# Two chunk pairs of the mixer's input and output products by seven products per unit, and a new order of the chunks around them

## The chip, the cores and the metric

One Trainium2 chip, one core of it. The metric is the device time of one execution in microseconds (us). Five engines work side by side and meet by semaphores: TensorE (PE; PEld is its weight load), VectorE (DVE), ScalarE (ACT), GpSimd (POOL) and SyncE (SP), which issues the DMAs of the weights.

## The reference, cut to what matters

A decoder layer for 256 tokens, width 2048, fp32: a SwiGLU FFN, a mixer, and a second SwiGLU FFN, each closed by `LayerNorm(alpha * x + sublayer(x))`. The mixer is where the change is:

```python
(c_q, c_kv, k_rope, q_nsa, k_c, v_c, k_s, v_s, k_w, v_w, g_nsa) = split_cols(x @ w_in[l], IN_SIZES)
o_mla = mla_attention(c_q, c_kv, k_rope, ...)      # latent attention, 8 heads
o_nsa = nsa_attention(q_nsa, k_c, v_c, ...)        # compressed, selected and window branches, 8 heads
mix = jnp.concatenate([o_mla, o_nsa], axis=-1) @ w_out[l]
x = layer_norm(DEEPNORM_ALPHA * x + mix, ln2_g[l], ln2_b[l])
```

`w_in` is 2048 x 3416: 512 columns c_q, 256 c_kv, 64 k_rope, 1024 q_nsa, six times 256 for the keys and values of the branches (compressed, selected, window), 24 gates. `w_out` is 2048 x 2048; its rows 0 to 1023 take the latent heads, its rows 1024 to 2047 the NSA heads. `compress` makes 15 keys and 15 values out of overlapping blocks of 32 tokens of k_c and v_c, with a 4096 x 256 weight each.

## The kernel before, in words

The 256 tokens are two tiles t of 128 rows. The activations stand transposed in pieces (k, t) of 128 x 128 and are the stationary operand; weights stream as 128 x 512. Every large product in fp32 is three matmuls (`mm3`: high by high, high by low, low by high), so each weight is split in two. A piece of weights is 128 x 1024, half a megabyte: two k's of a chunk of 512 columns. SP loads it into `raw` (5 buffers) or `sum` (3 buffers), ACT casts the high part `whi` (L91 in `split`) and DVE subtracts for the low part `wlo` (L92); `whi` and `wlo` have 6 buffers each, so the cast of a piece waits until TensorE is done with the piece that lay in its buffer six splits ago.

`gemm` makes one chunk for both tiles. `gemm2` makes two chunks at once and goes by units, a unit being a pair of k's by two chunks by two tiles. A normal unit is 8 products, 24 matmuls. A unit named in `seven` is 7 products, 21 matmuls, by sums: DVE makes sums of the weights (L293 to L295) and splits four tiles instead of two, sums of the activations are made once (`sums`, `parts`), and at the end three accumulations `p1`, `p5`, `p6`, `p7` are put together by one ACT copy and four DVE operations (L332 to L336) and added to the four results (L345). FFN chunks are done so already; in the mixer no product is.

The mixer runs after the first LayerNorm (`ln`, by steps that are spread among the matmuls): chunks of `w_in` in the order c_q (`fin_a`), `w_in_b` = c_kv, k_rope and gates (`fin_b`: RMS norm, rope, gates), the compressed keys and values (`fin_c`); then the latent queries, latent attention for heads 0 to 3, the selected branch, NSA queries and so on, and at last `w_out`. Small attention work is written as generators (`spawn`) that advance by `tick`, between pieces of the large products, so that their waits lie behind matmuls; `drain` runs all of them to their end. The order on PE and SP is the order in which the program is written. The order on DVE, ACT and POOL is made by the scheduler at build time and fixed. Each engine runs its list from the front.

`out_last` does the last chunks of `w_out` tile by tile, so that the second LayerNorm's work on tile 0 lies behind the matmuls of tile 1. `out_fin` adds a finished chunk to the residual y, `ln_stats` takes its statistics.

## Time and profile before

| | before |
|---|---|
| time, median of 3 runs | 1766.75 us (1765.04 to 1768.03) |
| the profiled execution: time, span of its instructions | 1766.0 us, 1764.3 us |
| TensorE busy | 1745.0 us, 99% of the span |
| VectorE busy | 1596.6 us, 90% |
| ScalarE busy | 997.8 us, 57% |
| GpSimd busy | 17.4 us, 1% |
| mean granted TensorE clock | 0.998 |
| mean DMA rate | 198 GB/s |

The profile is one execution. What lies outside the span is 1.7 us. A busy share is a mean over the whole program. The mixer with its two LayerNorms lies at about 690 to 1060 us of the span; there the shares of DVE and ACT are lower than in the FFNs.

### The profile page before, as it was taken

The page shows a single profiled execution, that of the slowest core. Times are in us where ns is not written, and L with a number is a line of the kernel's source. Part 1 is how long each engine was busy: PE and PEld are TensorE (multiplying, and loading weights), DVE is VectorE, ACT ScalarE, POOL GpSimd, SP SyncE. Part 2 cuts the span into 40 slices and gives each one's busy share as a digit, 9 for nine tenths or more (in the row PEclk, how much of TensorE's full clock was granted, in tenths as well). Part 3 has the DMA queues.
Part 4 walks back from the last instruction along what each step waited for, and adds up shares of the span by engine and source line. Part 5 has one row for each costly group of instructions (what it writes and reads, how often), then busy time and mean ns, then how long its engine had stood idle before and what let it go on. Part 6 is the DMA issues. An engine that isn't in the chain of part 4 may idle for free.

```text
span 1764.3 us, 22385 instructions
## 1 busy us (share of the span) xinstructions
PE 1745.0 (99%) x8018; PEld 1429.0 (81%) x8018; DVE 1596.6 (90%) x2121; ACT 997.8 (57%) x1324; POOL 17.4 (1%) x40
## 2 busy tenths in 40 slices
PE   9999999999999999999999999999999999999997
PEld 7888888888888888887788778888888888888886
DVE  7899999999999998766576679899999999999997
ACT  6656555575655565654555555565655565655651
POOL 0000000000000000000000001000000000000000
PEclk9999999999999999999999999999999999999999
DMA  9665656556567557546843355656556656566654
GB/s 335 219 209 176 209 200 203 192 189 211 196 197 230 193 177 255 182 143 210 300 153 120 123 176 171 211 179 198 196 193 224 203 185 209 196 196 216 203 197 162
DMA packets 103440, 350.01 MB, mean 198 GB/s; under 512 B 11152, under 2 KB 13728, under 8 KB 103328
## 3 DMA queue, kind: packets, MB, share of 16 engines
q1 hardware_dynamic: 102016, 344.37, 58.1%
q0 software_dynamic: 1312, 4.21, 0.8%
q8 instruction: 63, 1.03, 0.2%
q14 instruction: 49, 0.40, 0.1%
HBM read 346.44 MB, written 2.10 MB: 198 GB/s over the span
## 4 chain that ended last, share of the span: by engine, by line
PE 74%; DVE 17%; DMA 3%; issue 3%; ACT 2%; SPq 0%; POOL 0%; DVEq 0%; ACTq 0%; POOLq 0%
PE bank L97 23%; PE bank L98 23%; PE bank L96 23%; DVE wlo L92 8%; DVE sum L293 2%; DVE w L345 2%; ACT whi L91 1%; DMA raw<-in_ffn_w_down 1%; DVE sum L295 1%; DVE sum L294 1%; DMA raw<-in_ffn_w_up 1%; DVE tlo L448 1%; PE bank L1004 1%; DMA raw<-in_w_in 1%; PE bank L994 1%
## 5 line engine op out<-in xcount | busy, mean ns | idle before, releaser
L96 PE MATMUL bank<-whi,thi 128*128 128x512 f32 (+1 forms) x1958 | 771.9, 394 | 0.0
L97 PE MATMUL bank<-wlo,thi 128*128 128x512 f32 (+1 forms) x1958 | 761.2, 389 | 1.5 <-DVE wlo L92 1.4
L98 PE MATMUL bank<-whi,tlo 128*128 128x512 f32 (+1 forms) x1958 | 761.1, 389 | 0.0
L91 ACT CAST whi<-raw 128x1024 fp32r<-128x1024 f32 (+2 forms) x569 | 533.1, 965 | 264.7 <-PE bank L98 123.2
L92 DVE TENSOR_TENSOR wlo<-raw,whi 128x1024 fp32r<-128x1024 f32 (+2 forms) x569 | 624.0, 1111 | 63.6 <-ACT whi L91 62.9
L91 ACT CAST whi<-sum 128x1024 fp32r<-128x1024 f32 x267 | 279.2, 1050 | 369.3 <-DVE sum L295 143.2
L96 PEld LDWEIGHTS bank<-whi,thi 128*128 128x128 f32 x1958 | 368.0, 188 | 79.1 <-issue 5.4
L98 PEld LDWEIGHTS bank<-whi,tlo 128*128 128x128 f32 x1958 | 367.6, 188 | 76.5
L97 PEld LDWEIGHTS bank<-wlo,thi 128*128 128x128 f32 x1958 | 368.2, 188 | 75.8 <-DVE wlo L92 3.8
L92 DVE TENSOR_TENSOR wlo<-sum,whi 128x1024 fp32r<-128x1024 f32 x267 | 319.3, 1214 | 26.0 <-ACT whi L91 23.7
L97 PE MATMUL bank<-wlo,m 128*128 128x512 f32 x424 | 166.0, 392 | 2.0 <-DVE wlo L92 2.0
L96 PE MATMUL bank<-whi,m 128*128 128x512 f32 x424 | 165.1, 389 | 0.0
L98 PE MATMUL bank<-whi,m 128*128 128x512 f32 x424 | 165.1, 389 | 0.0
L293 DVE TENSOR_TENSOR sum<-raw 128x1024 f32<-128x1024 f32 x106 | 129.0, 1217 | 9.1 <-DMA raw<-in_ffn_w_down 5.0
L97 PEld LDWEIGHTS bank<-wlo,m 128*128 128x128 f32 x424 | 79.5, 188 | 22.3 <-DVE wlo L92 5.5
L96 PEld LDWEIGHTS bank<-whi,m 128*128 128x128 f32 x424 | 79.6, 188 | 16.6
L98 PEld LDWEIGHTS bank<-whi,m 128*128 128x128 f32 x424 | 79.6, 188 | 16.0
L345 DVE TENSOR_TENSOR w<-bank,w 128x512 f32<-128x512 f32 x120 | 78.7, 681 | 0.2
L295 DVE TENSOR_TENSOR sum<-sum,raw 128x512 f32<-128x512 f32 x106 | 72.3, 683 | 0.2
L294 DVE TENSOR_TENSOR sum<-sum,raw 128x512 f32<-128x512 f32 x106 | 72.3, 683 | 0.0
L733 ACT ACTIVATE w<-w,mx 128x256 f32<-128x256 f32 (+1 forms) x48 | 21.4, 446 | 29.8 <-DVE mx L729 28.1
L440 PEld LDWEIGHTS bank<-ident,w 128*128 128x128 f32 x176 | 21.9, 140 | 5.8
(190 smaller groups left out, 889.7 us busy)
## 6 DMA issues: line engine op xcount, KB each, us to landing
raw<-in_ffn_w_down SPq DMA_DIRECT2D x169, 512.0 KB, 4.7
raw<-in_ffn_w_up SPq DMA_DIRECT2D x160, 512.0 KB, 4.8
raw<-in_ffn_w_gate SPq DMA_DIRECT2D x146, 512.0 KB, 5.0
raw<-in_ffn_gu SPq DMA_DIRECT2D x32, 512.0 KB, 4.2
raw<-in_w_in SPq DMA_DIRECT2D x30, 512.0 KB, 5.1
raw<-in_w_out SPq DMA_DIRECT2D x20, 512.0 KB, 3.3
sum<-in_w_in SPq DMA_DIRECT2D x18, 512.0 KB, 5.4
sum<-in_ffn_w_gate SPq DMA_DIRECT2D x12, 512.0 KB, 4.1
```

The lines of the kernel that those rows point to most:

```text
L91: A.copy(hi, src)
L92: V.tensor_tensor(lo, src, f(hi), op=OP.subtract)
L96: PE.matmul(ps, xh, wh, start=first, stop=False)
L97: PE.matmul(ps, xh, wl, start=False, stop=False)
L98: PE.matmul(ps, xl, wh, start=False, stop=last)
L293: V.tensor_tensor(t13, a_, b_[:, 1:2, :].broadcast_to([P, 2, NCH]), op=OP.add)
L294: V.tensor_tensor(t24[:, 0], t13[:, 0], a_[:, 1], op=OP.add)
L295: V.tensor_tensor(t24[:, 1], t24[:, 0], b_[:, 0], op=OP.add)
L345: V.tensor_tensor(rest[b], B[b], rest[b], op=OP.add)
L440: PE.transpose(pt[:, j, :], hs[c, t][:, j * P:(j + 1) * P], ident)
L448: V.tensor_tensor(hT[c, t][1], src, f(hT[c, t][0]), op=OP.subtract)
L733: A.activation(s[:, h, :], s[:, h, :], AF.Exp, bias=mx[:, h:h + 1], accum_out=sm[:, h:h + 1])
```

## The change

- `w_in`: the chunk c_q and the chunk of the compressed keys and values become one pair, `w_in_a`, done by `gemm2` with units 4 and 5 by seven products. The first four units are done for tile 0 first, then for tile 1 (`head=4`). Before, c_q was a `gemm` with `head=8` and the other chunk came after `w_in_b`.
- The order after `w_in_b`: the compressing generators are spawned and the selected branch's chunk comes directly; then latent queries, the latent attention of heads 0 to 3, and the first NSA queries. Before: latent queries, latent attention, then the spawn and the selected branch.
- `w_out`: all four chunks are done for rows 0 to 1023 as before. For rows 1024 to 2047, columns 0 to 1023 become a pair `w_out_a` (`gemm2`, four units in the order 0, 1, 3, 2, of which 1 and 2 by seven products), and columns 1024 to 2047 are `w_out_b`, done whole in `out_last`. Before, rows 1024 to 1535 were done for all chunks, then came `drain`, rows 1536 to 2047 of chunk 0, and `out_last` did the other three.
- `drain` now runs in the pair, after its first unit (`mixed`), where the activations' sums for unit 2 are made too (`mix_sums`).
- `ln` makes the activations' sums of units 4 and 5 itself (`now_too`). The values of the second latent attention stand in a `sum` buffer.

```diff
+WIN, WIN7 = (0, 1, 2, 3, 4, 6, 5, 7), (4, 5)
+WOUT, WOUT7 = (0, 1, 3, 2), (1, 2)
...
+                    if now_too and len(u) == 4:
+                        xs[2 * n + j] = parts(sums(u))
...
-    gemm(xin, w_in, 0, KALL, fin_a, head=HEAD, spare=SPARE, nxt=(W["w_in_b"], 0, 0))
-    gemm(xin, W["w_in_b"], 0, KALL, fin_b, nxt=(w_in, 3, 0))
...
-    gemm(xin, w_in, 3, KALL, fin_c, nxt=(uq, 2, 0))
+
+    gemm2(xin, xs1, WIN, WIN7, "w_in_a", 0, lambda t, j, r: (fin_c if j else fin_a)(t, r), head=4,
+          nxt=(W["w_in_b"], 0, 0))
+    gemm(xin, W["w_in_b"], 0, KALL, fin_b, nxt=(w_in, 2, 0))
...
+    def out_last(w, ks):
 
         held = {}
         for t in range(NT):
-            for n in ns:
+            for n in range(2):
                 ps = new_bank()
                 if t == 0:
-                    held[n] = [(ks[i:i + KT], load(W["w_out"], n, ks[i:i + KT])) for i in range(0, len(ks), KT)]
+                    held[n] = [(ks[i:i + KT], load(w, n, ks[i:i + KT], n == 1 and i >= 4)) for i in range(0, len(ks), KT)]
...
-    gemm(lambda k, t: sl(cq[t], k), uq, 2, list(range(4)), fin_qr, nxt=(uq, 0, 0))
-    mla_att(*mla_proj(0, (w_in, 4, 0)))
     spawn(compress(kcT, "k"), "C")
     spawn(compress(vcT, "v"), "C")
     new_kv("sel")
-    gemm(xin, w_in, 4, KALL, fin_kv2("sel"), each=lambda i: ln_res("ln1", i // 2) if i % 2 else None,
-         nxt=(w_in, 1, 0))
+    gemm(xin, w_in, 2, KALL, fin_kv2("sel"), each=lambda i: ln_res("ln1", i // 2) if i % 2 else None, nxt=(uq, 2, 0))
+    gemm(lambda k, t: sl(cq[t], k), uq, 2, list(range(4)), fin_qr, nxt=(uq, 0, 0))
+    mla_att(*mla_proj(0, (w_in, 0, 0)))
...
-    out_proj(list(range(8)), range(4), True)
-    out_proj(list(range(8, 12)), range(4), False)
-    drain()
-    for n in range(1):
-        gemm(mixer, W["w_out"], n, list(range(12, 16)),
-             lambda t, ps: (out_fin(t, ps, n, False), ln_stats(t, n)))
-    out_last(list(range(12, 16)), (1, 2, 3))
+    for n in range(4):
+        gemm(mixer, W["w_out"], n, list(range(8)), lambda t, ps: out_fin(t, ps, n, True),
+             each=lambda i: mix_sums(1) if n == 3 and i == 2 else None)
+
+    def mixed(at):
+        if at == 0:
+            drain()
+            mix_sums(2)
...
+    gemm2(late_mix, xs3, WOUT, WOUT7, "w_out_a", 0, fin_o, each=mixed)
+    out_last(W["w_out_b"], list(range(8)))
```

In all there are 12 matmuls fewer, three for each of the four units of seven. The bytes loaded stay. The lines of `after` stand one to thirteen lines lower: `mm3` is L97 to L99, `split` L92 and L93, the sums L294 to L296, the putting together L333 to L337 and L348, the compressing matmuls L943, the softmax's transposes L774 and the products that follow them L1017, `out_fin` L1036.

Three places of the built order follow. First DVE, where the blocks for the first compressing matmuls are made (L919 before, L932 after). Before, at the end of the latent queries (L640 to L643 are rope, `wlo` the low parts of weights):

```order
L640 TENSOR_TENSOR w<-bank,pack 128x512
L643 TENSOR_TENSOR w<-w 128x512
L641 TENSOR_TENSOR w<-bank,pack 128x8x32
L642 TENSOR_TENSOR w<-bank,pack 128x8x32
L92 TENSOR_TENSOR wlo<-sum,whi 128x1024
L643 TENSOR_TENSOR w<-w 128x512
L92 TENSOR_TENSOR wlo<-sum,whi 128x1024 x2
L92 TENSOR_TENSOR wlo<-raw,whi 128x1024
L917 MEMSET w 128x32
L919 TENSOR_TENSOR w<-m,pack 128x16x15 x2
```

And after, right behind `w_in_b` (L659 to L662 the RMS norm of `fin_b`, L649 to L652 its rope, L689 to L692 the gates):

```order
L659 TENSOR_SCALAR ms<-ss 128x1
L93 TENSOR_TENSOR wlo<-raw,whi 128x1024
L687 COPY w<-w 128x64
L534 TENSOR_SCALAR rstd<-ms 128x1
L662 TENSOR_SCALAR w<-bank,rstd 128x256
L691 TENSOR_SCALAR gz<-gz 128x24
L684 MEMSET w 128x256
L692 RECIPROCAL gates<-gz 128x24
L649 TENSOR_TENSOR w<-bank,pack 128x64
...
L930 MEMSET w 128x32
L932 TENSOR_TENSOR w<-m,pack 128x16x15
```

The blocks have moved from behind rope and weight splits to behind the whole of `fin_b` for tile 1.

Second ACT, at the last softmax (L746 before, L756 after, scales the probabilities; L766 and L776 copy the transposed ones out of a bank; `whi` the high parts of weights). Before:

```order
L733 ACTIVATE w,sm<-w,mx 128x256 x2
L91 CAST whi<-sum 128x1024
L746 ACTIVATE w<-w,rs 128x256 x2
L91 CAST whi<-sum 128x1024
L766 COPY w<-bank 128x512
```

After, in the pair `w_out_a`:

```order
L92 CAST whi<-raw 128x1024
L743 ACTIVATE w,sm<-w,mx 128x256 x2
L92 CAST whi<-raw 128x1024
L756 ACTIVATE w<-w,rs 128x256 x2
L776 COPY w<-bank 128x512
```

The list of ACT is nearly the same; the cast between the exponentials and the scaling is now the one that waits for the buffer that the last matmul of unit 0 reads. On PE the transposes L774 and the products L1017 now follow that matmul back to back, where 12 matmuls stood between L764 and L1004.

Third DVE, from the end of `w_out_a` into `out_last` (L334 to L337 and L348 put the seven products together, L1036 adds to y, L541 is the statistics; the `wlo<-sum` is the second piece of the second chunk of `w_out_b`). After:

```order
L334 TENSOR_TENSOR w<-bank,w 128x512
L93 TENSOR_TENSOR wlo<-raw,whi 128x1024
L335 TENSOR_TENSOR w<-bank,w 128x512
L348 TENSOR_TENSOR w<-bank,w 128x512
L336 TENSOR_TENSOR w<-bank,w 128x512
L337 TENSOR_TENSOR w<-bank,w 128x512
L1036 TENSOR_TENSOR y_92<-w,y_92 128x512
...
L1036 TENSOR_TENSOR y_92<-bank,y_92 128x512
L541 BN_STATS bn_9356<-y_93 128x6
L541 BN_STATS bn_9349<-y_92 128x6
L93 TENSOR_TENSOR wlo<-sum,whi 128x1024
```

And the like place before, where `out_last` begins (L1023 adds to y, L538 is the statistics):

```order
L1023 TENSOR_TENSOR y_93<-bank,y_93 128x512
L92 TENSOR_TENSOR wlo<-sum,whi 128x1024 x2
L1023 TENSOR_TENSOR y_92<-bank,y_92 128x512
L1023 TENSOR_TENSOR y_93<-bank,y_93 128x512
L538 BN_STATS bn_9286<-y_92 128x6
L538 BN_STATS bn_9295<-y_93 128x6
L92 TENSOR_TENSOR wlo<-sum,whi 128x1024
```

Before, four short operations stand between two splits; after, 17 stand between the split of the second chunk's first piece and that of its second: L335, L336 and L337, four L348, five L1036 and five L541.

## Rows read from the trace of the kernel before

**Rows 1.** The page, engines: busy us, share of the span, instructions.

```profile
PE 1745.0 (99%) x8018; PEld 1429.0 (81%) x8018; DVE 1596.6 (90%) x2121; ACT 997.8 (57%) x1324; POOL 17.4 (1%) x40
```

**Rows 2.** Timeline of TensorE in an undisturbed stretch (start, busy us, engine, line, operation): the first and the last of 22 matmuls in a row, 21 steps.

```profile
1008.18 0.39 PE L98 MATMUL bank<-whi,tlo 128*128 128x512 f32 x1
...
1012.95 0.40 PE L98 MATMUL bank<-whi,tlo 128*128 128x512 f32 x1
```

**Rows 3.** Busy time by stretches of 50 us of the mixer (stretch, its us, then busy us and instructions of PE, PEld, DVE, ACT and POOL, granted clock, DMA share, GB/s).

```profile
700.00:750.00 50.00, 49.46 (x267) 43.05 (x265) 39.88 (x77) 33.30 (x55) 2.20 (x4) 1.00 0.57 181
750.00:800.00 50.00, 49.44 (x249) 40.17 (x247) 30.78 (x61) 24.49 (x46) 2.78 (x5) 1.00 0.45 152
...
1000.00:1050.00 50.00, 50.00 (x225) 40.98 (x224) 35.78 (x52) 22.87 (x34) 0.56 (x1) 1.00 0.47 158
1050.00:1100.00 50.00, 49.09 (x231) 40.23 (x230) 49.54 (x89) 31.33 (x48) 4.87 (x9) 1.00 0.51 172
```

**Rows 4.** The page, costliest groups: the sums of weights of a seven unit (busy us, mean ns).

```profile
L293 DVE TENSOR_TENSOR sum<-raw 128x1024 f32<-128x1024 f32 x106 | 129.0, 1217 | 9.1 <-DMA raw<-in_ffn_w_down 5.0
...
L295 DVE TENSOR_TENSOR sum<-sum,raw 128x512 f32<-128x512 f32 x106 | 72.3, 683 | 0.2
```

**Rows 5.** Timeline of TensorE at the end of the chunk of `w_in_b`: its last matmul and the first of the next chunk.

```profile
745.12 0.32 PE L98 MATMUL bank<-whi,tlo 128*128 128x344 f32 x1
745.28 0.40 PE L96 MATMUL bank<-whi,thi 128*128 128x512 f32 x1
```

**Rows 6.** Timeline of VectorE behind that chunk: the work of `fin_b` on both tiles (L650 to L683), with splits (L92) among it.

```profile
745.85 0.15 DVE L650 TENSOR_SCALAR ms<-ss 128x1 f32<-128x1 f32 x1
...
747.62 1.16 DVE L92 TENSOR_TENSOR wlo<-raw,whi 128x1024 fp32r<-128x1024 f32 x1
...
749.50 1.22 DVE L92 TENSOR_TENSOR wlo<-raw,whi 128x1024 fp32r<-128x1024 f32 x1
...
752.36 0.48 DVE L653 TENSOR_SCALAR w<-bank,rstd 128x256 f32<-128x256 f32 x1 [0.73 <-POOL rstd L532]
...
753.03 1.16 DVE L92 TENSOR_TENSOR wlo<-sum,whi 128x1024 fp32r<-128x1024 f32 x1
...
754.55 0.23 DVE L643 TENSOR_TENSOR w<-w 128x64 f32<-128x64 f32 x1
```

**Rows 7.** Groups by line over the mixer: the additions that make the compressing blocks.

```profile
L919 DVE TENSOR_TENSOR w<-m,pack 128x240 f32<-128x240 f32 x8 | 4.3, 562 | 0.0
```

**Rows 8.** The page, DMA issues of the mixer's weights (KB each, us from issue to landing).

```profile
raw<-in_w_in SPq DMA_DIRECT2D x30, 512.0 KB, 5.1
```

**Rows 9.** Timeline of ScalarE in the first latent attention.

```profile
819.19 1.04 ACT L91 CAST whi<-sum 128x1024 fp32r<-128x1024 f32 x1 [5.11 <-DMA sum<-in_w_in]
820.14 0.58 ACT L766 COPY w<-bank 128x512 f32<-128x512 f32 x1
```

**Rows 10.** Timeline of TensorE there.

```profile
819.04 0.39 PE L98 MATMUL bank<-whi,tlo 128*128 128x512 f32 x1
820.77 1.16 PE L852 MATMUL bank<-w,m 128*128 128x128 f32 x8 [1.35 <-ACT w L766]
```

**Rows 11.** Timeline of ScalarE at the last softmax.

```profile
1010.65 1.05 ACT L91 CAST whi<-sum 128x1024 fp32r<-128x1024 f32 x1 [0.20 <-PE bank L98]
1011.61 0.91 ACT L746 ACTIVATE w<-w,rs 128x256 f32<-128x256 f32 x2
...
1014.34 0.58 ACT L766 COPY w<-bank 128x512 f32<-128x512 f32 x1
```

**Rows 12.** Timeline of TensorE there: the last transposes, the first matmul behind them, and the products.

```profile
1013.18 0.60 PE L764 MATMUL bank<-ident,w 128*128 128x128 f32 x4
1013.54 0.48 PE L96 MATMUL bank<-whi,thi 128*128 128x512 f32 x1
...
1016.38 1.02 PE L1004 MATMUL bank<-w,m 128*128 128x256 f32 x4
```

**Rows 13.** Timeline of VectorE in `out_last`: two additions to y, two statistics, a split, an addition.

```profile
1036.04 1.28 DVE L1023 TENSOR_TENSOR y<-bank,y 128x512 f32<-128x512 f32 x2
1037.24 1.28 DVE L538 BATCH_NORM_STATS2 bn<-y 128x6 f32<-128x512 f32 x2
1038.43 1.21 DVE L92 TENSOR_TENSOR wlo<-sum,whi 128x1024 fp32r<-128x1024 f32 x1
1039.56 0.68 DVE L1023 TENSOR_TENSOR y<-bank,y 128x512 f32<-128x512 f32 x1
```

**Rows 14.** Timeline of TensorE at the second LayerNorm, where the gate's first matmuls begin.

```profile
1054.68 0.50 PE L96 MATMUL bank<-m,thi 128*128 128x512 f32 x1 [0.50 <-ACT thi L91]
...
1055.83 0.50 PE L98 MATMUL bank<-m,tlo 128*128 128x512 f32 x1 [0.41 <-DVE tlo L92]
```

**Rows 15.** Timeline of TensorE: the last matmul of the program.

```profile
1753.67 0.39 PE L98 MATMUL bank<-whi,tlo 128*128 128x512 f32 x1
```

**Rows 16.** Stretches behind that matmul (columns as in group 3).

```profile
1756.00:1760.00 4.00, 0.00 (x0) 0.00 (x0) 4.00 (x8) 0.00 (x0) 0.92 (x1) 0.76 0.29 110
1760.00:1764.30 4.30, 0.00 (x0) 0.00 (x0) 1.30 (x2) 0.00 (x0) 0.00 (x0) 0.50 0.38 142
```

**Rows 17.** Timeline of TensorE at the start of the program: the first of the products and the fifth.

```profile
5.07 0.80 PE L96 MATMUL bank<-whi,thi 128*128 128x512 f32 x1
...
7.17 0.40 PE L97 MATMUL bank<-wlo,thi 128*128 128x512 f32 x1
```

More of the change, by code (lines that the diff above doesn't have):

```diff
@@ L69, in layer @@
     W = {n: (a.get(n), (k // P) // KT, w) for n, (k, w) in _CHUNKS.items()}
[L70 removed]
+    W2 = {n: (a[n + "_2"], _CHUNKS[n][0] // P // KT) for n in _PAIRED}
     def am(dt=F32):
@@ L226, in gemm, with gemm2 @@
             at += 1
-    def gemm2(x, xs, kps, seven, w, cp, finish, each=None, head=0, pre=None):
+    def gemm2(x, xs, kps, seven, w, cp, finish, each=None, head=0, pre=None, nxt=None):
         src, pairs = W2[w]
@@ L342, in gemm2 @@
                 each(at)
+        if nxt:
+            ahead[id(nxt[0]), nxt[1], nxt[2]] = load(nxt[0], nxt[1], [nxt[2] + j for j in range(KT)])
         for b in [(t, j) for t in range(NT) for j in range(2)]:
@@ L579, in ln @@
             for j in range(2):
-                if xs is not None and 2 * n + j in UP7:
-                    xs.setdefault(2 * n + j, []).extend(v[:, 2 * j + i, :] for i in range(2))
+                if 2 * n + j in want:
+                    u = xs.setdefault(2 * n + j, [])
+                    u.extend(v[:, 2 * j + i, :] for i in range(2))
+                    if now_too and len(u) == 4:
+                        xs[2 * n + j] = parts(sums(u))
             yield 1
@@ L791, in mla_proj @@
     def mla_proj(g, nxt):
-        qnT, knT, vm = (am2() for _ in range(3))
+        qnT, knT = (am2() for _ in range(2))
+        m = am() if g == 0 else sump.tile([P, KT, NCH], F32, name="sum").rearrange("p k (a b) -> p (k a) b", b=P)
+        vm = m[:, 0:4, :], m[:, 4:8, :]
         knT = [k.rearrange("p (h t) q -> p h t q", h=2) for k in knT]
@@ L1023, in out_fin, with mix_sums @@
             V.tensor_tensor(y[t][:, cs], ps, y[t][:, cs], op=OP.add)
-    def out_proj(ks, ns, first):
-        for n in ns:
-            gemm(mixer, W["w_out"], n, ks, lambda t, ps: out_fin(t, ps, n, first))
-    x2, xs2 = {}, {}
-    def out_last(ks, ns):
+    x2, xs2, xs3 = {}, {}, {}
+    late_mix = lambda k, t: mixer(k + 8, t)
+    def mix_sums(i):
+        v = []
+        for t in range(NT):
+            hi, lo = mix[2 + i // KT, t]
+            u = wk([P, 2, P])
+            js = slice(i % KT * KT, (i % KT + 1) * KT)
+            V.tensor_tensor(u, f(hi[:, js, :]), f(lo[:, js, :]), op=OP.add)
+            v += [u[:, j] for j in range(KT)]
+        xs3[i] = parts(sums(v))
+    def out_last(w, ks):
         held = {}
         for t in range(NT):
-            for n in ns:
+            for n in range(2):
                 ps = new_bank()
                 if t == 0:
-                    held[n] = [(ks[i:i + KT], load(W["w_out"], n, ks[i:i + KT])) for i in range(0, len(ks), KT)]
+                    held[n] = [(ks[i:i + KT], load(w, n, ks[i:i + KT], n == 1 and i >= 4)) for i in range(0, len(ks), KT)]
                 for pc, wp in held[n]:
                     for k, (hi, lo) in zip(pc, wp):
-                        mm3(ps, mixer(k, t), hi, lo, k == ks[0], k == ks[-1])
+                        mm3(ps, late_mix(k, t), hi, lo, k == ks[0], k == ks[-1])
                     tick(1)
-                out_fin(t, ps, n, False)
-                ln_stats(t, n)
-            spawn(ln(t, "ln2", LN_EPS, x2, xs2))
+                out_fin(t, ps, 2 + n, False)
+                ln_stats(t, 2 + n)
+            spawn(ln(t, "ln2", LN_EPS, x2, xs2, UP7, False))
             steps()
     qrT += am2()
-    gemm(lambda k, t: sl(cq[t], k), uq, 2, list(range(4)), fin_qr, nxt=(uq, 0, 0))
-    mla_att(*mla_proj(0, (w_in, 4, 0)))
     spawn(compress(kcT, "k"), "C")
@@ L1101 @@
          ("ln2_b", 16), ("mla_q_norm_g", 4), ("mla_kv_norm_g", 2), ("pe_k", 32), ("pe_v", 32), ("w2_k", 256), ("w2_v", 256))
-_CHUNKS = {"w_in": (D, NCH), "w_in_b": (D, 344), "mla_w_uq": (QR, NCH), "mla_w_ukv": (KVR, NCH), "w_out": (D, NCH)}
+_CHUNKS = {"w_in": (D, NCH), "w_in_b": (D, 344), "mla_w_uq": (QR, NCH), "mla_w_ukv": (KVR, NCH), "w_out": (D // 2, NCH),
+           "w_in_a": (D, NCH), "w_out_a": (D // 2, NCH), "w_out_b": (D // 2, NCH)}
 for _n in ("ffn1", "ffn2"):
@@ L1108 @@
 _PAIRED = {f"{_n}_{_s}": _m for _n in ("ffn1", "ffn2")
-           for _s, _m in (("w_gate", 10), ("w_up", 10), ("w_down", 4), ("gu", 2))}
+           for _s, _m in (("w_gate", 10), ("w_up", 10), ("w_down", 4), ("gu", 2))} | {"w_in_a": 2, "w_out_a": 2}
 def kernel(**inputs):
@@ L1117 @@
     w = arr["w_in"]
-    cols = {"w_in": [(0, O_CKV), (O_Q, O_G)], "w_in_b": [(O_CKV, O_Q), (O_G, O_G + 24)]}
+    cols = {"w_in": [(O_Q, O_KC), (O_KS, O_G)], "w_in_a": [(0, O_CKV), (O_KC, O_KS)],
+            "w_in_b": [(O_CKV, O_Q), (O_G, O_G + 24)]}
     arr.update({n: np.concatenate([w[:, :, i:j] for i, j in c], 2) for n, c in cols.items()})
+    w = arr["w_out"]
+    h = D // 2
+    arr.update({"w_out": w[:, :h], "w_out_a": w[:, h:, :h], "w_out_b": w[:, h:, h:]})
     uq = arr["mla_w_uq"].reshape(1, QR, 8, HD + RD)
```

17 lines of the change are left out of this document (9 added, 8 removed).

## The prediction

> **What bounds the kernel now.** I read the busy times of the engines first. TensorE is busy 1745.0 of 1764.3 us [rows 1], so of the span only 19.3 us are not matmul, and 10 of these lie behind the last matmul, which begins at 1753.67 [rows 15], where the last LayerNorm and the output run. TensorE's list sets the time: a matmul taken away gives its slot, and a new wait costs its whole length. A slot is read from a stretch without waits: 21 steps from 1008.18 to 1012.95, 0.227 us each [rows 2]. The table by stretches then says who has room in the mixer: DVE is busy 39.88 and 30.78 of 50 us at its beginning and 35.78 near its end, but 49.54 of 50 right behind it [rows 3]. Last I read the places where TensorE stands still in the mixer. The longest shows how these waits come about: at 819.04 the last matmul before the latent attention's products begins, at 820.77 the products [rows 10]. They wait for ScalarE's copy at 820.14, and that stood behind a cast that waited 5.11 us for a DMA, though the copy itself needed nothing of it [rows 9]. So here a wait is made by what stands ahead in an engine's list, not by a lack of time on that engine.
>
> **What it saves.** Four units of 21 instead of 24 matmuls are 12 slots: 12 x 0.227 = 2.7 us. The additions that go with this on DVE and ACT lie beside matmuls. For `w_in_a`: a seven unit adds a sum of 1024 (1.22 us), two of 512 (0.68 each) [rows 4] and, a half piece less but two pieces more, about 1.9 us of splits, together 4.5; two units are 9 us. With the activations' sums and the putting together I estimate some 17 us over the 60 us between LayerNorm and the end of `w_in_b`, where DVE has 10 of 50 us free in the first stretch and 19 in the next [rows 3]. It fits with little to spare; I take 0, and at most 1.5 us if a split of units 5 or 6 comes late. The second LayerNorm has two waits today, 0.50 and 0.41 us, as its first gate matmuls are reached [rows 14]. There 48 matmuls instead of 36 will lie between tile 0's and tile 1's end, which is enough to cover them: I take -0.6 (0 to -0.9).
>
> **First wait, the compressing blocks.** Call E the end of `w_in_b`. After the change the first four compressing matmuls stand 24 slots later, at E + 5.4. They need two additions of 0.56 us [rows 7] that stand on DVE behind the whole of `fin_b`. Before, E is 745.28, one 344-column slot of 0.16 behind the start of the last matmul at 745.12 [rows 5], and `fin_b` runs on DVE from 745.85 to the rope's last addition at 754.55 [rows 6], E + 9.5 with its end. Three splits of 1.14 are in that (747.62, 749.50, 753.03); after the change one is, so it ends at E + 7.2. A memset (0.2, as the short operation at 754.55) and the two additions with a copy between them (1.3) make E + 8.7. The first norm can start some 0.8 us sooner than at 745.85, since no split stands right ahead of it: E + 7.9. The wait is thus 2.5 us. It grows if the split in the middle waits for its weights: its `raw` buffer comes free with the split of a piece whose cast waits for the matmul 36 slots of 0.16 before E; with cast and split (1.05 and 1.14) that is 3.3 us before E. A load takes 5.1 us in the median [rows 8] and the cast again 1.05, so the split starts at E + 2.9, some 0.5 us later than counted. I take 3.0 (1.5 to 6). Nothing was paid here before, since latent queries and attention came first.
>
> **Second wait, the drain.** In `w_out_a` the last softmax has unit 0's 24 matmuls as its only cover. Ahead of the scaling on ACT stands a cast into the buffer that the last of these 24 matmuls reads. Before, such a cast ran at 1010.65 and the scaling at 1011.61, and both were over before the transposes at 1013.18 [rows 11, 12]. Now the cast can begin only 0.2 us after unit 0's last slot, takes 0.96 to the next start, and the two scalings take 0.91 [rows 11]; with 0.1 for the semaphore the transposes are 2.15 late. Behind them the products come at once: transposes 0.60, copy 0.58, with two semaphores 1.3 us where a slot of 0.36 stood [rows 11, 12], so 0.9 more. Before, 12 matmuls, from 1013.54 to 1016.38, hid that [rows 12]. Together 3.1 (2 to 4).
>
> **Third wait, the second chunk of `out_last`.** Let E now be the end of `w_out_a`. Its last unit is a seven, so everything that puts it together falls on DVE at E, and `wlo` of the sixth piece (second of the second chunk) stands behind that. DVE starts on L334 at about E, then 0.6 for it, 1.14 for a split, then 17 operations on 512 columns. Such operations follow each other every 0.60 us: four from 1036.04 to 1038.43 [rows 13]. 17 x 0.60 = 10.2, and the split that is waited for takes 1.14 (1038.43 to 1039.56): done at E + 13.1. TensorE has 24 matmuls of the first chunk, 6 of the fifth piece and one more: it asks at E + 31 x 0.227 = 7.0. The wait is 6.1 (4.5 to 7). The later splits then come every 0.6 us for every 1.4 of matmuls, and cost nothing. Before, four such operations stood between two splits, not 17.
> The page PSUM — Partial Sum Buffer of the Trainium skill, section Engine vs sequencer instructions, says that the queues of ScalarE, VectorE and GpSimd are strict FIFO. The copy at 820.14 agrees [rows 9]. By that rule the sixth piece's split can't pass the 17 operations though its cast is done by E + 1.4, and the 6.1 us stand; if a list could be passed, the term would be 0.
>
> **Other moves, taken at nothing.** The latent attention of heads 0 to 3 now has the compressing of the values beside it and its loads; the wait there before (1.5 us at 819.04, and a shorter one) came from a late DMA, and I take it to be paid again: 0, from -2 to +3. Fewer additions to y (`w_out` in two parts for all columns) free DVE where it isn't waited for; the cover is already there.
>
> **Sum.** 1766.0 - 2.7 - 0.6 + 3.0 + 3.1 + 6.1 = 1774.9; the median of the runs is 0.75 above this profiled execution, so I say 1775.
>
> **Rivals.** (a) *The third wait doesn't come* (not slower). If the work at the end of `w_out_a` is over in time, 6.1 us go and the time is 1769, within 0.2% of before. For it, the operations between E + 1.74 and the split would have to fit in 4.15 us, 0.24 each; the shortest step seen for such an operation is 0.60 [rows 13]. So it needs a scheduler's list other than the one shown. (b) *Both attention waits are hidden*, by `fin_b` running ahead and the cast finding its buffer free sooner: 1775 - 6.1 = 1769, also within 0.2%. For the first the blocks would have to be ready at E + 5.4 instead of 7.9, which the two waits for GpSimd of 0.7 in `fin_b` [rows 6] speak against. (c) *All three are hidden* and only the matmuls count: 1763.4, faster. (d) *The loads become the bound* where compressing and latent attention now meet: a cast that waits on a load as at 819.19 [rows 9] stands ahead of the attention's copies twice instead of once, 2 to 5 us more: 1777 to 1780. For it: the 5.11 us wait there exists; against: the bytes are the same and no stretch shows DMA at its limit. (e) *The clock falls during the third wait.* In the tail, without matmuls, the granted clock is 0.92 from 1756 to 1760 and 0.50, the lower level of 1.2 GHz, from there on [rows 16]. At the start of the program four products took from 5.07 to 7.17 [rows 17], 2.1 us instead of 0.9, so a fall may cost 1.2 us, twice that if eight are slow: 1776 to 1778.
> The page TensorE: Matmul & The Clock Gate, section What's actually happening, states the two levels and that the lower one is the default to which an idle engine returns; by it a 6 us wait is a place where (e) can happen. The waits in the mixer before, up to 1.5 us, show no fall: the granted clock is 1.00 in every stretch [rows 3].
>
> **How the numbers follow.** A change of under 0.2% (3.5 us) can't be told from none here. Chances: the forecast, 1770.5 to 1779, 0.60; (a) 0.08; (b) 0.07; (c) 0.05; (d) 0.13; (e) 0.07. Slower is forecast, (d) and (e), 0.80; same (a) and (b), 0.15; faster (c), 0.05. The range goes from just below (a) and (b) with the lower bounds of other terms, 1767, to the upper end of (d), 1780.5.
>
> **What would show it.** The changed profile should have 12 matmuls fewer on L97 to L99 together, and three waits of TensorE: at the first L943 for DVE (L932), at the last L774 for ACT (L756), with L1017 for L776 behind it, and one of some 6 us at L98 in `out_last` for `wlo`. The steps are wrong if one of these is under half its size, if TensorE waits in `w_in_a` for a split, or if the time grows in the FFNs, where nothing was changed.

## The result, and the profile after

The changed kernel takes 1789.85 us in the median (1786.03 to 1793.59, five runs) against 1766.99 us before, measured beside it: a ratio of 1.0126 (1.0116 to 1.0137). It is 22.9 us slower; 8 us were forecast. The profiled execution of after took 1792.05 us, its span 1790.3 us, 26.0 more than the span before.

The engines of after, from the page (busy us, share, instructions), as [rows 1] of before:

```profile
PE 1753.4 (98%) x8006; PEld 1433.8 (80%) x8006; DVE 1624.8 (91%) x2173; ACT 1007.4 (56%) x1338; POOL 18.4 (1%) x40
```

TensorE has the 12 matmuls less (8006, not 8018), and is yet busy 8.4 us longer: its matmuls have become slower. The stretches of the mixer, columns as in [rows 3], show where:

```profile
800.00:850.00 50.00, 47.66 (x262) 35.66 (x261) 30.54 (x55) 25.01 (x50) 0.00 (x0) 0.97 0.59 213
850.00:900.00 50.00, 47.62 (x242) 38.25 (x241) 28.20 (x44) 27.25 (x56) 0.00 (x0) 0.93 0.52 192
950.00:1000.00 50.00, 47.38 (x228) 37.79 (x226) 33.98 (x69) 25.55 (x62) 0.00 (x0) 0.97 0.27 85
1000.00:1050.00 50.00, 47.25 (x202) 37.02 (x201) 35.06 (x58) 28.71 (x49) 0.00 (x0) 0.97 0.42 147
1050.00:1100.00 50.00, 41.56 (x185) 33.69 (x184) 43.07 (x85) 23.80 (x40) 3.27 (x6) 0.90 0.43 140
```

The granted clock, third column from the right, was 1.00 in every stretch of before's mixer and is 0.90 to 0.97 in these five. In the FFNs ahead of 700 and behind 1100 us it is 1.00, as before, and nothing is lost there. All that TensorE waits for between 690 and 1110 us, by line and releaser (us in total, times, longest):

```profile
PE bank L98 <- DVE wlo L93: 7.9, 3, 6.3
PE bank L97 <- ACT whi L92: 3.1, 2, 1.6
PE bank L993 <- DVE pc L758: 2.6, 1, 2.6
PE bank L548 <- DVE y L578: 2.2, 1, 2.2
PE bank L943 <- DVE w L932: 2.0, 1, 2.0
PE bank L774 <- ACT w L756: 1.9, 2, 1.5
...
```

With one of 0.7 (L1017) and two of 0.3 these are 21.0 us; the same view of before has 3.9. So of the 26.0 us, 17.1 are more waiting, 2.7 are saved by the 12 slots, and 11.6 remain for the clock and the short restart behind each wait. That fits the stretches: one minus the clock, times 50 us, summed over the five, is 0.03 + 0.07 + 0.03 + 0.03 + 0.10 of 50 us = 13.0, an upper bound since part of it fell into the waits themselves (from 1058 to 1060, inside the longest wait, the granted clock is 0.50). This execution is one of the longer ones; by the medians about 8.5 us remain, if the waits are the same in the others. Their granted clock over the whole span is low too: 0.991 to 0.994 in the five runs of after, 0.997 to 0.999 in those of before that stand beside the experiments.

The three waits that were forecast, on TensorE's timeline (start, busy us, line, [wait <- releaser]):

```profile
773.01 0.39 PE L99 MATMUL bank<-whi,tlo 128*128 128x512 f32 x1
775.44 0.64 PE L943 MATMUL bank<-raw,w 128*32 128x256 f32 x8 [2.04 <-DVE w L932]
...
1026.33 0.39 PE L99 MATMUL bank<-whi,tlo 128*128 128x512 f32 x1
1028.27 0.95 PE L774 MATMUL bank<-ident,w 128*128 128x128 f32 x4 [1.55 <-ACT w L756]
1029.89 1.22 PE L1017 MATMUL bank<-w,m 128*128 128x256 f32 x2 [0.68 <-ACT w L776]
...
1054.22 0.39 PE L97 MATMUL bank<-whi,thi 128*128 128x512 f32 x1
1060.86 0.80 PE L98 MATMUL bank<-wlo,thi 128*128 128x512 f32 x1 [6.25 <-DVE wlo L93]
```

Start to start, less the slot, they cost 2.2 us; 1.7 and then 1.3 (1.62 less the 0.36 that the transposes take without a wait); and 6.4 us. The four that were not forecast:

```profile
809.24 0.50 PE L97 MATMUL bank<-whi,thi 128*128 128x512 f32 x1 [1.46 <-ACT whi L92]
810.62 0.50 PE L98 MATMUL bank<-wlo,thi 128*128 128x512 f32 x1 [0.88 <-DVE wlo L93]
...
865.27 0.50 PE L97 MATMUL bank<-whi,thi 128*128 128x512 f32 x1 [1.62 <-ACT whi L92]
866.53 0.79 PE L98 MATMUL bank<-wlo,thi 128*128 128x512 f32 x1 [0.76 <-DVE wlo L93]
867.12 0.63 PE L99 MATMUL bank<-whi,tlo 128*128 128x512 f32 x1
867.55 0.63 PE L97 MATMUL bank<-whi,thi 128*128 128x512 f32 x1
...
985.72 1.01 PE L993 MATMUL bank<-ident,pc 128*15 128x128 f32 x4 [2.62 <-DVE pc L758]
...
1086.80 0.66 PE L548 MATMUL bank<-ident,y 128*128 128x128 f32 x4 [2.18 <-DVE y L578]
```

They are 9.5 us of waiting. Behind the second pair of waits, at 865, the matmuls follow each other every 0.43 us (867.12, 867.55) where [rows 2] had 0.227; thirteen steps up to 872.7 are of that kind.

### The profile page after: what moved, and what is told of

Read it like the earlier page. It is cut to its first block, busy times and chain, and to the rows that moved or that the text cites. A ratio compares the mean times of both kernels' runs of the same rounds, so it can differ in the third digit from the quotient of the medians.

```text
span 1790.3 us, 22413 instructions
## 1 busy us (share of the span) xinstructions
PE 1753.4 (98%) x8006; PEld 1433.8 (80%) x8006; DVE 1624.8 (91%) x2173; ACT 1007.4 (56%) x1338; POOL 18.4 (1%) x40
## 4 chain that ended last, share of the span: by engine, by line
PE 77%; DVE 15%; DMA 3%; issue 3%; ACT 2%; POOL 0%; SPq 0%; DVEq 0%; ACTq 0%; POOLq 0%
PE bank L98 24%; PE bank L99 24%; PE bank L97 24%; DVE wlo L93 6%; DVE sum L294 1%; DVE w L348 1%; ACT whi L92 1%; DVE sum L296 1%; DVE sum L295 1%; DMA raw<-in_ffn_w_down 1%; PE bank L1017 1%; DMA raw<-in_ffn_w_up 1%; DMA raw<-in_mla_w_uq 1%; DVE tlo L451 1%; PE bank L443 1%
## 5 line engine op out<-in xcount | busy, mean ns | idle before, releaser
L97 PE MATMUL bank<-whi,thi 128*128 128x512 f32 (+1 forms) x1930 | 764.1, 396 | 3.8 <-ACT whi L92 3.8
L99 PE MATMUL bank<-whi,tlo 128*128 128x512 f32 (+1 forms) x1930 | 753.0, 390 | 0.0
L92 ACT CAST whi<-raw 128x1024 fp32r<-128x1024 f32 (+2 forms) x576 | 538.7, 963 | 271.8 <-PE bank L99 147.3
L93 DVE TENSOR_TENSOR wlo<-raw,whi 128x1024 fp32r<-128x1024 f32 (+2 forms) x576 | 630.6, 1110 | 58.0 <-ACT whi L92 57.5
L92 ACT CAST whi<-sum 128x1024 fp32r<-128x1024 f32 (+1 forms) x266 | 277.9, 1051 | 355.1 <-DVE sum L296 146.2
L97 PEld LDWEIGHTS bank<-whi,thi 128*128 128x128 f32 x1930 | 364.3, 189 | 80.9 <-ACT whi L92 5.9
L99 PEld LDWEIGHTS bank<-whi,tlo 128*128 128x128 f32 x1930 | 364.2, 189 | 75.9
L93 DVE TENSOR_TENSOR wlo<-sum,whi 128x1024 fp32r<-128x1024 f32 (+1 forms) x266 | 318.2, 1216 | 24.2 <-ACT whi L92 22.2
L98 PE MATMUL bank<-wlo,m 128*128 128x512 f32 x440 | 172.1, 391 | 1.9 <-DVE wlo L93 1.9
L97 PE MATMUL bank<-whi,m 128*128 128x512 f32 x440 | 171.3, 389 | 0.0
L99 PE MATMUL bank<-whi,m 128*128 128x512 f32 x440 | 171.3, 389 | 0.0
L294 DVE TENSOR_TENSOR sum<-raw 128x1024 f32<-128x1024 f32 x110 | 134.1, 1219 | 8.6 <-DMA raw<-in_ffn_w_up 4.9
L97 PEld LDWEIGHTS bank<-whi,m 128*128 128x128 f32 x440 | 82.8, 188 | 17.4
L99 PEld LDWEIGHTS bank<-whi,m 128*128 128x128 f32 x440 | 82.6, 188 | 16.7
L348 DVE TENSOR_TENSOR w<-bank,w 128x512 f32<-128x512 f32 x128 | 84.5, 683 | 0.8 <-PE bank L99 0.5
L296 DVE TENSOR_TENSOR sum<-sum,raw 128x512 f32<-128x512 f32 x110 | 75.3, 685 | 0.1
L295 DVE TENSOR_TENSOR sum<-sum,raw 128x512 f32<-128x512 f32 x110 | 75.3, 685 | 0.0
```

The lines of the kernel that those rows point to most:

```text
L92: A.copy(hi, src)
L93: V.tensor_tensor(lo, src, f(hi), op=OP.subtract)
L97: PE.matmul(ps, xh, wh, start=first, stop=False)
L98: PE.matmul(ps, xh, wl, start=False, stop=False)
L99: PE.matmul(ps, xl, wh, start=False, stop=last)
L294: V.tensor_tensor(t13, a_, b_[:, 1:2, :].broadcast_to([P, 2, NCH]), op=OP.add)
```

## What stands ahead of each unforeseen wait

**809 and 865.** Two lists stand ahead of the weights of the latent queries, SP's and ACT's. SP's DMA issues of after:

```profile
787.64 0.33 SPq L168 DMA_DIRECT2D raw<-in_mla_w_uq  x1
801.73 0.33 SPq L947 DMA_DIRECT2D w<-in_pack  x1
802.10 0.43 SPq L168 DMA_DIRECT2D raw<-in_mla_w_uq  x1
...
852.16 0.43 SPq L168 DMA_DIRECT2D sum<-in_mla_w_uq  x1
```

From issue to landing (us, last column), the loads of 802.10 and of 852.16:

```profile
raw<-in_mla_w_uq SPq DMA_DIRECT2D x1, 512.0 KB, 3.9
sum<-in_mla_w_uq SPq DMA_DIRECT2D x1, 512.0 KB, 4.6
```

What SP's queue waited for between 780 and 860 us, among others:

```profile
SPq L947 <- PE bank L943: 13.7, 1, 13.7
SPq L947 <- PE bank L774: 6.8, 1, 6.8
```

The DMA of L947 brings the small second weight of `compress` into a work buffer that the last of the L943 matmuls still reads. For 14 us SP issues nothing, and the loads of the latent weights stand behind it though they go into other buffers. The second such DMA was issued at 851.78, and the next piece of the latent weights right behind it. But the pieces were there before they were cast: that of 802.10 landed at 806.0, that of 852.16 at 856.8. What comes last is ACT's list. At 809 two copies for the keys (L892) stand in front of the cast and wait for the transposes at 807.18; at 865 it is the cast of activations `thi`, which waits for the products at 862.60 (L865).

```profile
807.60 0.65 ACT L892 COPY m<-bank 128x256 f32<-128x256 f32 x2 [2.77 <-PE bank L891]
808.13 2.95 ACT L92 CAST whi<-raw 128x1024 fp32r<-128x1024 f32 x3
...
863.69 0.58 ACT L92 CAST thi<-bank 128x512 fp32r<-128x512 f32 x1 [2.77 <-PE bank L865]
864.17 2.94 ACT L92 CAST whi<-sum 128x1024 fp32r<-128x1024 f32 x3
```

The first cast is over at 809.2 and TensorE goes on at 809.24; at 865 it is over at 865.2 and TensorE goes on at 865.27. Begun as its piece landed, the first cast (about 1.05 us) would have been over at 807.1 and 857.9, before TensorE asked (about 807.8 and 863.6). Whether ACT's list has this order because the scheduler reckoned with late loads isn't shown. Before, pieces of `w_in` stood behind this DMA (it was issued at 827.39 and 864.71), and TensorE waited for none of them; it is the new order that puts the latent loads there.

**985.** DVE, ahead of the scaled probabilities `pc` that L993 transposes:

```profile
982.57 1.23 DVE L294 TENSOR_TENSOR sum<-raw 128x1024 f32<-128x1024 f32 x1
...
984.22 1.23 DVE L93 TENSOR_TENSOR wlo<-sum,whi 128x1024 fp32r<-128x1024 f32 x1 [0.34 <-ACT whi L92]
985.36 0.21 DVE L758 TENSOR_TENSOR pc<-pc,rs 128x60 f32<-128x60 f32 x1
```

L294 is the sum of weights of the first seven unit of `w_out_a`, which TensorE reaches some 40 us later. Why the scheduler put it into the list here isn't shown.

**1086.8.** DVE ahead of the second LayerNorm's normalizing of tile 1:

```profile
1081.29 0.68 DVE L1036 TENSOR_TENSOR y<-bank,y 128x512 f32<-128x512 f32 x1
1081.89 1.22 DVE L93 TENSOR_TENSOR wlo<-sum,whi 128x1024 fp32r<-128x1024 f32 x1
1083.02 1.29 DVE L93 TENSOR_TENSOR tlo<-w,thi 128x512 fp32r<-128x512 f32 x2
1084.23 0.69 DVE L541 BATCH_NORM_STATS2 bn<-y 128x6 f32<-128x512 f32 x1
...
1086.21 1.00 DVE L578 TENSOR_SCALAR y<-y,mv,rstd 128x512 f32<-128x512 f32 x2
```

The last addition to tile 1's y is followed by three splits of weights and activations before its statistics are taken; TensorE asked at 1084.5.

## The experiments

My theory was that each of these waits is made by what stands ahead in one engine's list, and that the clock falls behind the longer ones. The rivals were a lack of time on DVE, by which waits only change place, and an error in the forecast waits. All ratios are against the kernel before, measured beside the run.

**The halves.** One kernel has only the edits to `w_in` and the order behind it, the other only those to `w_out`:

```diff
-    gemm2(late_mix, xs3, WOUT, WOUT7, "w_out_a", 0, fin_o, each=mixed)
-    out_last(W["w_out_b"], list(range(8)))
+    out_proj(list(range(8)), range(4), True)
```

```diff
-    gemm2(xin, xs1, WIN, WIN7, "w_in_a", 0, lambda t, j, r: (fin_c if j else fin_a)(t, r), head=4,
+    gemm(xin, w_in, 0, KALL, fin_a, head=HEAD, spare=SPARE, nxt=(W["w_in_b"], 0, 0))
```

> Only the input half of the change (w_in_a by sevens, the new order of compressing, latent queries and attention, the values in a sum buffer); w_out and out_last as before. My theory, that each place of the changed trace pays by itself (six matmuls fewer, 1.4 us; the waits at the first compressing matmul 2.2, at the latent attention's first weights 4.4 with the slow slots behind them instead of 2.2 before, at the second attention's first weights 6.5): 1767.0 + 8 to 10, so 1775 to 1777. Rival, that the whole loss comes from the output half and the waits in front are only moved slack: at most 1769. Second rival, that losses multiply (a late front makes the back late): under 1773 here and more than the rest in the output half alone.

> Only the output half (w_out_a by sevens, drain after its first unit, out_last over all late rows for the last two chunks); w_in and the order as before. My theory: six matmuls fewer (1.4 us), waits at the second NSA softmax 4, at the drain 4.5, at the sixth piece of out_last 8 with its slow slots, at the second LayerNorm 3 more: 1767.0 + 17, so 1782 to 1786. Rival, that the three waits of the prediction alone count: 1767 + 8, 1775. The two halves together should give the whole, 22.9 us, if places pay independently.

The input half took 1772.4 us, 1.0030 (1.0019 to 1.0041), and has the waits at 775, 809 and 864. The output half took 1785.4, 1.0099 (1.0082 to 1.0116), with the waits of pc (2.6), of the drain, of `out_last` (6.25) and at the second LayerNorm (2.2). The parts add up to 1.29%, the whole is 1.26%: neither half's loss is seen to hang on the other. The second rival's first sign, under 1773, is met, but its second, more than the rest in the output half, is not beyond the intervals (18.7 us where 17.2 were left). The input half was cheaper than expected, by 3 us: its clock stayed at 0.996 to 0.998. It waits 8.1 us where before waits 3.9, saves six slots (1.4 us) and is 5.7 us slower, so some 2.8 us come on top of the waits' length.

**The old order kept**, with both pairs in place:

```diff
+    gemm(lambda k, t: sl(cq[t], k), uq, 2, list(range(4)), fin_qr, nxt=(uq, 0, 0))
+    mla_att(*mla_proj(0, (w_in, 2, 0)))
     spawn(compress(kcT, "k"), "C")
...
-    gemm(lambda k, t: sl(cq[t], k), uq, 2, list(range(4)), fin_qr, nxt=(uq, 0, 0))
-    mla_att(*mla_proj(0, (w_in, 0, 0)))
```

> All of the change but the order of the mixer's middle: latent queries and the first latent attention come before the compressing again, as before. My theory: the waits at the first compressing matmul (2.2), at 809 (4.4) and at 865 (6.5) go, and the attention's wait of before (2.2) comes back: 1789.9 - 11, so 1778 to 1780. Rival, that sevens in w_in_a cost DVE time that is paid somewhere in the mixer anyway: 1785 or more.

1787.0 us, 1.0111 (1.0096 to 1.0126): a miss by 7 us. The waits at 775, 809 and 865 are gone. The wait of before ahead of the attention's products [rows 10] is back with 1.22 us (827), as expected, and others have come: 1.97 us for `thi` at 785.89, and two for the rope of `fin_b` (0.62 and 0.31) at 780. On ACT the cast of that `thi` (785.43) stands behind a cast that waited 2.44 us for the matmul at 783.53, and behind a copy. The old order pays in another place; the order was not the fault by itself.

**The small weight on another queue.**

```diff
-        nc.sync.dma_start(w2.rearrange("p m d -> p (m d)"), cst["w2_" + n])
+        G.dma_start(w2.rearrange("p m d -> p (m d)"), cst["w2_" + n])
```

> All of the change, but the two small loads of the compressing's second weight (128 x 256) are issued from GpSimd's queue instead of SyncE's. My theory: on SyncE's list each of them waits for a work buffer and holds back the weight loads of the latent attention, so that the waits at 809 and 865 go: 1789.9 - 8 to 11, 1779 to 1782. Rival, that DMA bandwidth is short where compressing and latent attention meet: the pieces land as late as before and it stays at 1787 to 1790.

1785.6 us, 1.0104 (1.0089 to 1.0119). Both waits for `whi` are gone, so moving this load removes them, but 4 us were gained where 8 to 11 were expected: two waits of 0.41 and 1.42 us for the last steps of `compress` came instead (L952 and L967, for ACT), and less of the clock came back than I had put down to these places. In this kernel the casts also stand elsewhere in ACT's list, each soon after its piece has landed (at 801.38 ahead of the copies, at 847.52 far ahead of the last `thi`, 862.64). So the run shows that the load's queue decides, but not by which way: through late pieces, as the theory has it, or through the list that was built around them. The landing times above speak for the list.

**The units of `w_out_a` in the order 0, 1, 2, 3**, so that its last unit is a normal one and the putting together of the sevens is done 24 matmuls earlier:

```diff
-WOUT, WOUT7 = (0, 1, 3, 2), (1, 2)
+WOUT, WOUT7 = (0, 1, 2, 3), (1, 2)
```

> All of the change, but the units of w_out_a in the order 0, 1, 2, 3, so that a normal unit of 24 matmuls follows the last seven. Theory of the list (the sixth piece's split stands behind 17 finishing operations): these now run beside unit 3, and the split waits only for the addition of the first chunk of out_last, so the wait falls from 6.25 us to about 2, with fewer slow slots behind it: 1789.9 - 5 to 7, 1783 to 1785. Rival, that the weights of w_out_b land late and set the wait: 6 us stay and 1788 to 1791.

1779.2 us, 1.0063 (1.0047 to 1.0080). The wait of 6.25 becomes 2.67, that at the second LayerNorm 0.79, the drain 0.8 and 0.7. All waits fall by 6.4 us, to 14.6, the time by 10.7, some 4 us more than expected; of that 2.5 are the waits at the drain and at the second LayerNorm, which the expectation had not counted.

**The wait filled.** In the 6.25 us wait TensorE does 24 matmuls into a bank that nobody reads:

```diff
+                    if t == 0 and n == 1 and i == 1:
+                        scr = new_bank()
+                        for _ in range(24):
+                            PE.matmul(scr, late_mix(0, 0)[0], held[1][0][1][0][0], start=True, stop=True)
```

> All of the change, and 24 matmuls more of 128x512 into an unused bank right where TensorE waits 6.25 us in out_last; their results are not read. Theory that a wait also costs afterwards because the granted clock has fallen: with 5.4 us of the wait filled, the wait for DVE shrinks to under 1 us, the clock stays up there, and the time falls by 1 to 3 us in spite of 24 matmuls more: 1787 to 1789. Rival, that the slow slots behind waits are no matter of the clock at this place: 1790 or more, as the fillers' end and the bank they take can only delay.

1783.2 us, 1.0099 (1.0084 to 1.0114), against 1.0126 for the kernel without them: needless work makes it about 5 us faster, more than the 1 to 3 expected. TensorE's timeline there:

```profile
1049.74 5.60 PE L1064 MATMUL bank<-whi,thi 128*128 128x512 f32 x24
1055.18 0.39 PE L97 MATMUL bank<-whi,thi 128*128 128x512 f32 x1
1056.38 0.50 PE L98 MATMUL bank<-wlo,thi 128*128 128x512 f32 x1 [0.81 <-DVE wlo L93]
1056.71 0.39 PE L99 MATMUL bank<-whi,tlo 128*128 128x512 f32 x1
1056.94 0.39 PE L97 MATMUL bank<-whi,thi 128*128 128x512 f32 x1
```

The filling takes 5.44 us and the wait shrinks by as much, to 0.81. The steps behind it are 0.23 at once, where after has 0.43 (1061.45 and on). From 1050 to 1100 us the granted clock is 1.00 where after has 0.90. Of the waits, that at the second LayerNorm shrinks from 2.18 to 0.80 and one at 810 grows from 0.88 to 1.95, so by waits and filling together TensorE loses only 0.7 us less than in after; the rest of the 5 us goes with the clock. How much of it belongs to the filled wait alone is not shown: in this profiled execution the clock also stays at 1.00 behind the same waits at 865 and at 985 (1.62 with 0.76, and 2.61 us), behind which it fell in after.

**Four products of `out_last` ahead of the pair**, as cover for the last attention:

```diff
+    gemm(late_mix, W["w_out_b"], 0, [0, 1, 2, 3], lambda t, ps: out_fin(t, ps, 2, False))
     gemm2(late_mix, xs3, WOUT, WOUT7, "w_out_a", 0, fin_o, each=mixed)
...
+                ks = ks0 if n else ks0[4:]
```

> All of the change, but the first four late rows of the third chunk of w_out (24 matmuls) are done ahead of w_out_a instead of in out_last, so the last softmax has 48 matmuls behind it before the drain. Theory: the drain's 4.5 us go nearly whole; as the loads of w_out_a come later, the scheduler's list has no weight sum in front of the second NSA softmax, so its wait of 2.6 us goes too (3.5 with what follows); the sixth piece's wait stays at 4 to 6: 1789.9 - 8, 1780 to 1784. Rival, that the softmax waits come from the softmax's own chain: 1787 or more.

1782.1 us, 1.0084 (1.0069 to 1.0099). L294 no longer stands before `pc`, and the wait at 985 is gone; of the drain 1.7 us are left; `out_last`'s wait is 4.5.

**The mends together.** The first kernel has the other queue, the unit order and the cover of the runs above, `yield 4` instead of `yield 2` in `compress`, by which its first products come two steps later, and two steps more of delay (the first line of the diff) ahead of the second LayerNorm's transposes. The next leaves that delay out, so that four mends remain:

```diff
-        yield DLN
+        yield DLN + (2 if name == "ln2" else 0)
...
-        yield 2
+        yield 4
```

> All of the change with five edits for the waits: the small loads of the compressing on GpSimd's queue, its first matmul two pieces later, 24 matmuls ahead of w_out_a, units 0, 1, 2, 3, and the second LayerNorm's transposes two ticks later. If each wait is a matter of its place in a list, little is left: the first compressing wait (2.2), the weights of the attention (11 in the slow case), the NSA softmax (4), the drain (4.5), the sixth piece (6) and LayerNorm (3) go but for 3 to 6 us, 1763 to 1769. Rival, that they are replaced by others as VectorE's total work in the mixer is the limit: 1775 or more.

> e8 without the edit in the second LayerNorm (there the scheduler is told of two more slots of delay, and a wait of 3.21 us for thi on L97 came with it). My theory, that each wait is made by what stands ahead in one engine's list and can be mended there alone: that wait goes back to 0.8 us or less, as in e5, and the slow matmuls behind it go; 1772.4 - 2.4 - 1 = about 1769 (1767 to 1771). Rival, that waits only move from place to place and the sum of them is set by DVE's load: a wait of 2 to 3 us appears elsewhere, 1772.

With the delay 1772.4 us, 1.0033 (1.0023 to 1.0042), a miss: the delay makes a wait of its own.

```profile
1056.42 0.50 PE L97 MATMUL bank<-m,thi 128*128 128x512 f32 x1 [3.21 <-ACT thi L92]
```

Without it 1767.1 us, 1.0001 (0.9992 to 1.0011). All of the 23 us are back, though the 2.7 us of the saved slots do not show yet. What TensorE waits for in that kernel between 690 and 1110 us:

```profile
PE bank L98 <- DVE m L93: 2.4, 2, 2.2
PE bank L548 <- DVE y L578: 1.0, 1, 1.0
PE bank L98 <- DVE wlo L93: 1.0, 1, 1.0
...
```

With two of 0.3 these are 5.0 us, against 21.0 in after and 3.9 before. DVE has the same work as in after (1624.0 us busy against 1624.8), so DVE's load was not the bound: the rival by which waits only change place falls for their sum. The clock is 1.00 again in every stretch of 50 us from 800 to 1100 but one (0.97, behind the 2.2 us wait).

**Two steps on from there.** The statistics of the first two chunks are taken at the end of each tile in `out_last`, and then also the residual scalings of the first LayerNorm, whose own loads DVE waits for ahead of a split, go to the first NSA queries:

```diff
             out_fin(t, ps, 2 + n, False)
             ln_stats(t, 2 + n)
+        for n in range(2):
+            ln_stats(t, n)
...
-    gemm(xin, w_in, 2, KALL, fin_kv2("sel"), each=lambda i: ln_res("ln1", i // 2) if i % 2 else None, nxt=(uq, 2, 0))
+    gemm(xin, w_in, 2, KALL, fin_kv2("sel"), nxt=(uq, 2, 0))
```

> As e9, and in out_last the LayerNorm statistics of the first two chunks are taken later, so that m splits no longer stand behind them on DVE. Theory: the wait of 2.18 us on L98 for m in out_last falls under 1 us; 1767 (1765 to 1769). Rival: the statistics then fall into the time of the last chunk, where DVE puts its pieces together, and the wait before the second LayerNorm's matmuls grows by the same 1 to 2 us; 1769 or more.

> As e10, and the four scalings of the first LayerNorm's residual (ln_res of ln1, with the loads of its weights) go from the first piece of the compressing to the first of the queries. Theory: the wait of 1.74 us at 789 for wlo on L98, which stands behind a DVE operation that waits for those loads, goes; 1765 (1762 to 1768), and with the 12 matmuls saved the change would then be no slower than the kernel before (1766.5). Rival: the same operations delay the splits of the query pieces, 1 to 2 us there; no difference from e10.

1766.4 us, 1.0000 (0.9989 to 1.0011), and 1765.9 us, 0.9993 (0.9983 to 1.0002). The first took the wait of 2.2 out of `out_last`, and one of 2.19 came at 1059, in the second LayerNorm: the rival of that run was right. The second removed the wait at 790 (1.1 us in the run before it), and 1.9 us for ACT came around 850. Neither is told apart from the kernel before.

**The last long wait.** In the second LayerNorm ScalarE takes three of four scalings:

```diff
-            elif j % 2:
+            elif j if bcol is cst.get('ln2_b') else j % 2:
```

> As e11, and in the second LayerNorm ScalarE takes three of every four scalings of a transposed piece instead of two, because in e11 the one long wait left (2.19 us on L98 for wlo, at 1061) stands behind a stretch in which DVE has no idle time. Theory: that split then stands 8 places further ahead in DVE's list and the wait falls under 0.6 us: 1763.5 (1761.5 to 1766), about 0.2% under the kernel before. Rival: ScalarE, with 1.3 us more per tile in the same place, becomes the one that is late (a wait for thi on L97 of 1 to 2 us): 1765 or more, no difference from e11.

1763.7 us (11 runs), 0.9983 (0.9974 to 0.9992): 3 us faster than the kernel before, near what the 12 matmuls are worth. No wait is above 0.75 us:

```profile
PE bank L99 <- DVE tlo L93: 0.8, 2, 0.5
PE bank L98 <- DVE wlo L93: 0.7, 1, 0.7
...
```

This last edit is not bound to the change; what it would do to the kernel before was not tried.

## Why the prediction was wrong

The sign was right, for the reasons given: a list that decides what comes first, and work in front of what is waited for. The size was not.

By the signs that the prediction set for its steps they were right: 12 matmuls fewer, the three waits each over half their size, no new wait in `w_in_a`, and FFNs that are as long as before within 1.3 us. What failed are the terms that it put at nothing or below it.

- **What it saves: right.** 12 matmuls fewer. The 1.5 us for a late split in `w_in_a` did not come; TensorE waits there for nothing new.
- **First wait, 3.0: 2.2**, at the place and for the releaser named. The count without a late load gave 2.5; the 0.5 put on top, for a split that waits for its weights, did not come (on DVE the split at 770.40 waits for nothing). By the prediction's own numbers that buffer comes free 3.6 us before E, not 3.3 (36 x 0.16 less 1.05 and 1.14). **Second, 3.1: 3.0**, its parts 1.7 and 1.3 where 2.15 and 0.9 were reckoned: the transposes begin at 1028.27, when the first of the two scalings (0.90 for both, from 1027.71) is done, and take 0.95 where [rows 12] has 0.60. **Third, 6.1: 6.4.** DVE's 17 short operations every 0.60 us stood there as counted; the first of them and the split behind the last:

```profile
1049.43 0.69 DVE L335 TENSOR_TENSOR w<-bank,w 128x512 f32<-128x512 f32 x1
...
1059.60 1.21 DVE L93 TENSOR_TENSOR wlo<-sum,whi 128x1024 fp32r<-128x1024 f32 x1
```

From 1049.43 to 1059.60 are 10.2 us, the number of the sum. The three waits together are 11.6 where 12.2 was said.
- **"Other moves, taken at nothing": failed, +4.7 us of waiting at 809 and 865.** Since the two waits of before that were to be paid again (1.35 and 0.55) went, the waits make +2.8, just under the term's upper end of +3; the thirteen slow steps behind 865 alone are 2.6 more. Rival (d) had the place and a size of 2 to 5 us, but another cause, casts that wait for loads ahead of copies. What came is copies, and a cast of activations, ahead of the weights' casts, and bandwidth doesn't explain it: between 798 and 802 us the DMA engines move nothing at all. What the prediction didn't do is walk the moved step past the lists that it issues into, SP's, where one small DMA waits for a work buffer, and ACT's.
- **"Fewer additions to y free DVE", and the sums of `w_out_a` at nothing: failed, +2.6 us at 985.** Sums with 40 us to spare were taken for harmless. They stand in a fixed list, and what is behind them there was due at once.
- **The second LayerNorm, −0.6: failed, +2.2 us in place of the 0.9 of [rows 14].** Counting the 48 matmuls between the two tiles' ends was right for tile 0, whose waits are gone. It left out tile 1: its last addition, and the statistics behind that, now stand among splits on DVE for 5 us, and TensorE was done with the cover before.
- **Rival (e), the clock: right that it falls, wrong by far in the number of places and in its chance; in the sum it stood at nothing.** 1.2 to 2.4 us were given, for one wait, and there they held: behind the third wait eight matmuls take 3.35 us (1060.86 to 1064.21) where eight slots are 1.8. But 8.5 to 11.6 were paid, over six places in five stretches, at 865 alone 3.0 (fourteen steps, 866.53 to 872.67, 6.14 us where 3.2 would do). The text held that waits up to 1.5 us show no fall and looked only at the longest. In after the level falls behind 1.46 and 0.88 us in a row (809) as well: from 812 to 814 it is 0.50. And [rows 16] were misread: from 1756 to 1760 the granted clock is 0.76, third column from the right; 0.92 is GpSimd's busy time. No term of the sum hangs on it.

In numbers: 8.9 us were summed above the profiled execution, 26.0 came, 17.1 more. Waits not foreseen are 9.5 of it and the clock (with the short restart behind each wait) 11.6. Some 4 us stand against these: the forecast waits, without their restarts, are 10.5 where 12.2 were summed, and small waits of before went that were not claimed, the 1.35 of [rows 10] and two of 0.5 among them. What stays open is how far SP's queue shaped ACT's list at 809 and 865, and how the clock's loss divides among the single waits, since it differs from one execution to the next.

## What to carry to other kernels

When a step moves, walk it past every list it issues into, the DMA queue too, and ask of each entry in front what that waits for; a load that needs nothing can stand behind a small one that does, and a cast whose piece has landed behind a copy. A wait of TensorE can cost more than its length: in after six places with waits of 1.5 to 6 us cost some 1.5 to 3 us more each, while behind one of 2.04 (775) the clock did not fall. So price the clock for each wait in the sum, not for the longest alone. A saving of 12 slots is worth having only if the lists around it are put in order too: here four edits of order brought the time back to that of before, and three more 0.17% below it.
